# A hybrid RWKV-7 / sparse-attention / expert layer on one core: fewer gathered rows per v tile, more of them beside the weight matrix, eight low parts on GpSimd, four more unsplit v tiles

## The chip, the cores and the metric

The kernel runs on one core of one Trainium2 chip. The metric is device microseconds of one execution. Five engines run side by side, each through its own instruction stream in a fixed order: PE multiplies matrices, DVE, ACT and POOL (GpSimd) work on vectors, SP issues DMAs; POOL issues the gathering DMAs here as well. An instruction starts when those ahead of it in its stream have started and the semaphores that it waits for have come. A long wait at the head of a stream holds up everything behind it.

## The reference, cut to what matters

The layer has three parts: projections with RWKV-7 mixing and sparse attention, a gated output projection, and PEER, a layer of 16384 small experts. The change touches PEER alone:

```python
def block(hb):                       # 128 tokens
    q = (hb @ w_pq).reshape(PEER_BLOCK, PEER_HEADS, 2, PEER_DHALF)
    s = jnp.einsum('nhpd,hpkd->nhpk', q, peer_keys)
    ...                              # top 16 of 128 x 128 products of keys, by head
    e = jnp.take_along_axis(cidx, j, axis=-1)
    g = jax.nn.softmax(sc, axis=-1)
    act = jax.nn.gelu(jnp.einsum('nhkd,nd->nhk', peer_u[e], hb))
    return jnp.einsum('nhk,nhkd->nd', (g * act), peer_v[e])
```

There are 384 tokens of 1024 numbers. Each token has 8 heads of 16 chosen experts, 128 in all, and adds up 128 rows of `peer_v`, each weighted by a gate and by the gelu of a dot product with a row of `peer_u`.

## The kernel before

The 384 tokens are served in two ways at once.

**The sparse way** serves the 128 tokens of the sample group, one token a partition. In step q each token fetches its q-th expert: one indirect DMA, issued by POOL (L1603), brings 128 rows of 2048 numbers (u and v side by side, 1 MB). Here such a step is called a row. For each row DVE makes a dot product (L1610), ACT the gelu and the gate's factor (L1611, L1612), and DVE adds the scaled v half to an accumulator (L1616). There are 128 rows. They land in a ring of three buffers (`raw`), and late in the program also in parts of the large tile `G` that have become free.

**The dense way** serves the 256 prompt tokens with all experts, as if every token had chosen each of them with a weight that is mostly zero. The 16384 experts are 128 tiles of 128. For a u tile PE computes h2 times u (`dense_u`, L1501 on), ACT applies gelu. The weight matrix (`weights`, 64 groups of four tokens) is built from one-hot vectors by DVE and ACT and by small matmuls, and multiplied into the gelu values. For a v tile (`dense_v`) PE multiplies the weighted values with v and adds the result up in four banks `bx`, `cp`, `dx`, `dx` of PSUM over all 128 tiles.

A product in full precision goes to PE in one of two forms. Unsplit ("whole"), the operands are read as they are, and each matmul takes two passes. Split, ACT writes a rounded high part (`wh`, `Gh`; L238), another engine subtracts it for a low part (`wl`, `Gl`; L242), and PE makes three cheaper products, high x high, high x low and low x high. Of a v tile that is 12 matmuls of 512 columns, against 4 of two passes each.

The order around the change, in `run`:

- u tiles 0 to 41 unsplit, u tiles 42 to 75 split; from tile 30 on every tile pulls `SR[0]` = 0.5 rows.
- The weight matrix: 64 groups. After each group `ahead` (the step) makes half a u tile on average (`UR` = 0.5, tiles of the list `AHEAD`: 31 of the tiles from 76 on) and pulls `SR[1]` rows.
- 128 v tiles in an order that mixes early and late ones; their place is n. Before each, `SR[2]` rows are pulled; from n = 5 on a row may start only when the v tile five places ahead is done (`self.pace`, L1603's wait for PE). The 21 u tiles that are left go in between. A v tile is unsplit if n < 3, or if 8 < n < `EARLY` and n is divisible by 3.
- At n = 122 rows that are still left are pulled at once, and the sample tokens' result is written. The last two v tiles are finished bank by bank (`finish_v`), so that DVE can add the residual (L1586, L1587) of one bank while PE works on the next.

The order in which a program's instructions enter each engine's stream is set when the kernel is built, by a scheduler with a model of time of its own; so a change in one place moves instructions around it. The split's buffers are four for `wh`, three for `wl`, and three each for `Gh` and `Gl`.

Of the kernel before, what the change touches and what calls it, by code (L numbers as in the profile page):

```python
# [179 lines left out]

N1, NW, NA, NB = 42, 76, 8, 24
SCORES, TURNS = 18, (21, 39)
SR, UR = (0.5, 0.5, 0.62), 0.5
S0, PH = 30, 4
OFF = [j for j in range(NW, 128) if (j - NW + 1) * NB // (128 - NW) > (j - NW) * NB // (128 - NW)]
AHEAD = sorted(OFF + [j for j in range(NW, 128) if j not in OFF][:NA - 1])
LAST, EARLY = 126, 108
FREED = {}
for _k in "RWRWRWW":
    _a = max((j + 1 for j in FREED), default=0)  # L190
    FREED[_a + (7 if _k == "R" else 3)] = (_k, _a)
WB, EB = (4, 4, 3), 3
UENG, VENG, GENG, VN = 'v', 'v', 'g', 3
SENG = 'gv'
HENG, EENG, OB = 'va', 'vg', 3

# [5 lines left out]
class K:  # L202
# [1298 lines left out]
    def dense_u(self, j):  # L1501

        nc = self.nc
        u = self.expert(self.I["puT"][j].rearrange("p k e -> p (k e)"))
        p = self.ps([128, 256], tag="mm" if j < N1 and j % 2 else "u")
        if j < N1:
            u = u.rearrange("p (k e) -> p k e", k=8)
            for k in range(8):
                self.ulast = self.mm(p, u[:, k], self.h2f[:, k], start=(k == 0), stop=(k == 7))
        else:  # L1510
            uh, ul = (x.rearrange("p (k e) -> p k e", k=8) for x in self.split(u, UENG[j % len(UENG)]))
            hi, lo = self.h2p
            for k in range(8):
                self.mm(p, uh[:, k], hi[:, k], start=(k == 0), stop=False)
                self.mm(p, uh[:, k], lo[:, k], start=False, stop=False)
                self.mm(p, ul[:, k], hi[:, k], start=False, stop=(k == 7))
        off = j in OFF
        g = self.G[:, j] if j < NW else self.t([128, 256], tag="gO" if off else "gA", bufs=2 if off else NA, pool=self.late)
        nc.scalar.activation(g, p, AF.Gelu_apprx_tanh)
        if off:  # L1520
            nc.sync.dma_start(self.Ad[OFF.index(j)], g)
        return g
# [273 lines left out]
```

## Time and profile before

| | us |
|---|---|
| median of 3 runs | 1746.16 (1745.84 to 1750.6) |
| the profiled execution | 1751.29 |
| its span, first to last instruction | 1749.5 |
| one weight group's last instructions end, v tiles begin | about 1285 |
| last row is issued | 1693 |
| last matmul ends | 1744.7 |

The granted PE clock is 0.984 on average. Times below are microseconds from the start of the span. A line of groups reads: source line, engine, operation, what it writes and reads, shape, count, then busy time, mean nanoseconds of one, idle time of the engine just before them and what ended it. Most matmuls share L234, since one helper records them all; they are told apart by their tiles (`fx` of split u tiles, `bx`, `cp`, `dx` of v tiles).

### The profile page before, as it was taken

To read this page: it belongs to the slowest core of one execution; us is meant where nothing else is said; L and a number is where in the kernel's file an instruction comes from. 1 tells how busy PE (TensorE), PEld (TensorE's weight loads), DVE (VectorE), ACT (ScalarE), POOL (GpSimd) and SP (SyncE) were. 2 spreads that over 40 slices of the span, in tenths; PEclk is the share of its full clock that TensorE was granted. 3 is DMA by queue.
4 is the path that set the end of the run, shared out by engine and by line. 5 is a ranking of instruction groups with operands and counts; after the bars stand their busy time and mean duration, and the time that the engine had idled before them with its cause. 6 is when DMAs were issued, how large, how long until landed. Compare 5 with 4: busy or idle time off the path is not lost.

```text
span 1749.5 us, 33109 instructions
## 1 busy us (share of the span) xinstructions
PE 1671.5 (96%) x12376; PEld 1411.1 (81%) x12376; DVE 1358.9 (78%) x2905; ACT 744.2 (43%) x1666; POOL 550.2 (31%) x621
## 2 busy tenths in 40 slices
PE   6999899999999988999999989999999999999997
PEld 3998788878878877899887889999965776776675
DVE  3548888878858865566999998899957887777797
ACT  4443343333333333444323254577844433343343
POOL 2534243343323220035033223342233334332331
PEclk7999899999999999999999999999999999999999
DMA  8543653455365365755398989997579999999993
GB/s 294 171 133 104 195 177 89 146 173 158 103 202 157 98 210 178 261 184 195 126 358 320 366 322 372 390 330 242 175 257 357 380 385 370 392 394 375 351 396 111
DMA packets 173049, 437.23 MB, mean 250 GB/s; under 512 B 46036, under 2 KB 86612, under 8 KB 156504
## 3 DMA queue, kind: packets, MB, share of 16 engines
q1 hardware_dynamic: 154456, 300.89, 50.6%
q0 software_dynamic: 18432, 134.23, 19.8%
q8 instruction: 98, 1.61, 0.4%
q14 instruction: 63, 0.52, 0.1%
HBM read 403.75 MB, written 31.30 MB: 249 GB/s over the span
## 4 chain that ended last, share of the span: by engine, by line
PE 63%; DVE 17%; DMA 8%; issue 6%; ACT 3%; POOL 2%; SPq 0%; DVEq 0%; POOLq 0%; ACTq 0%
PE mm L234 23%; PE fx L234 12%; PE dx L234 11%; PE cp L234 7%; PE bx L234 7%; DVE acc L1616 2%; DVE wl L242 2%; DMA raw<-in_puv,pe 2%; DVE raw L1610 2%; DMA w<-in_w_in 1%; ACT wh L238 1%; DMA w<-in_puT 1%; POOL raw L1603 1%; DMA w<-in_pv 1%; DVE ps L1331 1%
## 5 line engine op out<-in xcount | busy, mean ns | idle before, releaser
L242 DVE TENSOR_TENSOR wl<-w,wh 128x1024 fp32r<-128x1024 f32 x231 | 291.5, 1266 | 94.3 <-ACT wh L238 55.3
L238 ACT ACTIVATE wh<-w 128x1024 fp32r<-128x1024 f32 x239 | 250.3, 1051 | 156.7 <-PE mm L234 70.9
L1603 POOL DMA_INDIRECT raw<-in_puv,pe x100 | 136.0, 1360 | 335.9 <-DVE acc L1616 118.0
L234 PE MATMUL fx<-h2h,wl 128*128 128x256 f32 x688 | 195.3, 285 | 3.9 <-DVE wl L242 3.8
L234 PE MATMUL fx<-h2h,wh 128*128 128x256 f32 x688 | 196.6, 286 | 0.9 <-ACT wh L238 0.7
L234 PE MATMUL fx<-h2l,wh 128*128 128x256 f32 x688 | 193.5, 281 | 0.0
L1616 DVE SCALAR_TENSOR_TENSOR acc<-raw,dots,acc 128x1024 f32<-128x1024 f32 x99 | 129.4, 1307 | 8.6 <-ACT dots L1612 8.5
L234 PEld LDWEIGHTS fx<-h2h,wl 128*128 128x128 f32 x688 | 130.3, 190 | 6.4 <-DVE wl L242 5.4
L234 PEld LDWEIGHTS fx<-h2h,wh 128*128 128x128 f32 x688 | 129.6, 188 | 5.6 <-ACT wh L238 2.7
L1610 DVE SCALAR_TENSOR_TENSOR raw<-raw,sh 128x1024 f32<-128x1024 f32 x100 | 125.4, 1254 | 7.4 <-DMA raw<-in_puv,pe 7.2
L234 PEld LDWEIGHTS fx<-h2l,wh 128*128 128x128 f32 x688 | 129.8, 189 | 1.6 <-issue 1.2
L234 PE MATMUL mm<-LTh,wh 128*128 128x384 f32 (+2 forms) x352 | 124.1, 353 | 2.1 <-ACT wh L238 1.5
L234 PE MATMUL mm<-LTh,wl 128*128 128x384 f32 (+2 forms) x352 | 123.2, 350 | 0.6 <-DVE wl L242 0.6
L234 PE MATMUL mm<-LTl,wh 128*128 128x384 f32 (+2 forms) x352 | 122.5, 348 | 0.0
L234 PE MATMUL mm<-h2f,w 128*128 128x256 f32 x464 | 105.4, 381 | 0.0
L1611 ACT ACTIVATE dots<-dots 128x1 f32<-128x1 f32 x128 | 25.4, 199 | 178.7 <-DVE raw L1610 149.5
L234 PE MATMUL mm<-wh,LTh 128*128 128x256 f32 x336 | 98.0, 292 | 1.7 <-ACT qx L898 1.7
L234 PE MATMUL mm<-wl,LTh 128*128 128x256 f32 x336 | 99.0, 295 | 0.0
L234 PE MATMUL mm<-wh,LTl 128*128 128x256 f32 x336 | 97.6, 290 | 0.0
L234 PEld LDWEIGHTS mm<-h2f,w 128*128 128x128 f32 x464 | 87.5, 190 | 12.4
L234 PE MATMUL fx<-h2f,w 128*128 128x256 f32 x336 | 78.3, 386 | 0.0
L234 PEld LDWEIGHTS mm<-LTh,wh 128*128 128x128 f32 (+2 forms) x352 | 66.7, 189 | 7.6 <-ACT wh L238 2.9
(609 smaller groups left out, 4475.8 us busy)
## 6 DMA issues: line engine op xcount, KB each, us to landing
w<-in_puT SPq DMA_DIRECT2D x119, 512.0 KB
w<-in_pv SPq DMA_DIRECT2D x85, 512.0 KB
w<-in_w_in SPq DMA_DIRECT2D x70, 512.0 KB
w<-in_w_ada SPq DMA_DIRECT2D x48, 512.0 KB
G<-in_pv SPq DMA_DIRECT2D x43, 512.0 KB
cKT<-in_cKT SPq DMA_DIRECT2D x32, 256.0 KB
cV<-in_cV SPq DMA_DIRECT2D x32, 256.0 KB
w<-in_w_pq SPq DMA_DIRECT2D x16, 512.0 KB
```

The source lines that it names most:

```text
L234: return self.nc.tensor.matmul(out, l, r, start=start, stop=stop, skip_group_check=True, **kw)
L238: self.nc.scalar.activation(hi, src, AF.Copy)
L242: (self.nc.vector if eng == "v" else self.nc.gpsimd).tensor_tensor(lo, src, hi, op=OP.subtract)
L1331: nc.vector.match_replace(out=s2, in_to_replace=sv[:, half, h, 0:8], in_values=s[:, c], imm_value=MARK)
L1603: d = nc.gpsimd.indirect_dma_start(out=bass.AP(tensor=u.tensor, offset=u.offset, ap=[u.ap[0], [1, 2048]]), out_offset=None, in_=self.I["puv"],
L1610: nc.vector.scalar_tensor_tensor(u, u, 1.0, h2, op0=OP.mult, op1=OP.mult, accum_out=dot)
L1611: nc.scalar.activation(dot, dot, AF.Gelu_apprx_tanh)
L1616: nc.vector.scalar_tensor_tensor(acc, v, dot, acc, op0=OP.mult, op1=OP.add)
```

## The change

Four numbers and one expression are changed. Rows beside the weight groups go from 0.5 to 0.57 a group, rows per v tile from 0.62 to 0.545. `EARLY` goes from 108 to 120, so the v tiles at n = 108, 111, 114 and 117 are no longer split. The low part of a split u tile is made by DVE before; now those at places 2, 6, 10 ... 30 of `AHEAD`, eight of 31, are made by POOL.

```diff
-SR, UR = (0.5, 0.5, 0.62), 0.5
+SR, UR = (0.5, 0.57, 0.545), 0.5
...
-LAST, EARLY = 126, 108
+LAST, EARLY = 126, 120
...
-UENG, VENG, GENG, VN = 'v', 'v', 'g', 3
+VENG, GENG, VN = 'v', 'g', 3
...
-            uh, ul = (x.rearrange("p (k e) -> p k e", k=8) for x in self.split(u, UENG[j % len(UENG)]))
+            uh, ul = (x.rearrange("p (k e) -> p k e", k=8) for x in self.split(u, "g" if j in AHEAD and AHEAD.index(j) % 4 == 2 else "v"))
```

The rows pulled in the program by the end of the weight groups are 55 before (6 with u tiles 30 to 41, 17 with tiles 42 to 75, 32 with the groups) and 59.48 now. The first five v tiles pull without a wait for PE: 58.1 before, 62.2 now.

On POOL's stream beside the weight groups, `G<-G,wg` (L1433) multiplies a group's weights into the gelu values, `raw<-in_puv,pe` (L1603) issues a row, `wl` (L242) is a low part. Before:

```order
L1603 DMA raw_15224<-in_puv,pe_2057_10521 128x2048
L1433 TENSOR_TENSOR G_11076<-G_11076,wg_13467 128x76x4
L1603 DMA raw_15258<-in_puv,pe_2057_10521 128x2048
L1433 TENSOR_TENSOR G_11076<-G_11076,wg_13533 128x76x4
L1603 DMA raw_15284<-in_puv,pe_2057_10521 128x2048
L1433 TENSOR_TENSOR G_11076<-G_11076,wg_13600 128x76x4
L1603 DMA raw_15303<-in_puv,pe_2057_10521 128x2048
L1433 TENSOR_TENSOR G_11076<-G_11076,wg_13673 128x76x4
L1603 DMA raw_15332<-in_puv,pe_2057_10521 128x2048
L1433 TENSOR_TENSOR G_11076<-G_11076,wg_13740 128x76x4
```

The same place of POOL's stream now:

```order
L1603 DMA raw_14920<-in_puv,pe_2057_10521 128x2048
L242 TENSOR_TENSOR wl_13268<-w_13264,wh_13267 128x1024
L1433 TENSOR_TENSOR G_11076<-G_11076,wg_13407 128x76x4
L1603 DMA raw_14987<-in_puv,pe_2057_10521 128x2048
L1433 TENSOR_TENSOR G_11076<-G_11076,wg_13474 128x76x4
L1603 DMA raw_15061<-in_puv,pe_2057_10521 128x2048
L242 TENSOR_TENSOR wl_13548<-w_13544,wh_13547 128x1024
L1603 DMA raw_15118<-in_puv,pe_2057_10521 128x2048
L1433 TENSOR_TENSOR G_11076<-G_11076,wg_13540 128x76x4
L1433 TENSOR_TENSOR G_11076<-G_11076,wg_13607 128x76x4
L1603 DMA raw_15185<-in_puv,pe_2057_10521 128x2048
```

The low parts stand right behind row issues, so they start after whatever those wait for.

On DVE's stream at the end of the program, L1610 and L1616 are the two halves of a row, L242 the low parts of v tiles (`wl`) and of their weighted values (`Gl`), L1586 the residual. Before, the last row is followed by five v tiles' low parts:

```order
L1616 SCALAR_TENSOR_TENSOR acc_11701<-G_11076,dots_18511,acc_11701 128x1024
L1586 TENSOR_TENSOR G_11076<-acc_11701,G_11076 128x512 x2
L242 TENSOR_TENSOR wl_18631<-w_18628,wh_18630 128x1024
L242 TENSOR_TENSOR Gl_18704<-G_11076,Gh_18703 128x256
L242 TENSOR_TENSOR wl_18676<-G_11076,wh_18675 128x1024
L242 TENSOR_TENSOR wl_18700<-G_11076,wh_18699 128x1024
L242 TENSOR_TENSOR wl_18721<-G_11076,wh_18720 128x1024
L242 TENSOR_TENSOR Gl_18728<-gB_18724,Gh_18727 128x256
L242 TENSOR_TENSOR Gl_18751<-gA_18028,Gh_18750 128x256
L242 TENSOR_TENSOR wl_18746<-w_18743,wh_18745 128x1024
L242 TENSOR_TENSOR wl_18756<-G_11076,wh_18755 128x1024
L242 TENSOR_TENSOR Gl_18763<-gB_18759,Gh_18762 128x256
```

Now the last three rows stand among the low parts of the last two v tiles:

```order
L242 TENSOR_TENSOR wl_18682<-w_18679,wh_18681 128x1024
L242 TENSOR_TENSOR Gl_18687<-gA_18009,Gh_18686 128x256
L1610 SCALAR_TENSOR_TENSOR G_11076,dots_18547<-G_11076,sh_2289_11699 128x1024
L242 TENSOR_TENSOR wl_18692<-G_11076,wh_18691 128x1024
L1616 SCALAR_TENSOR_TENSOR acc_11701<-G_11076,dots_18547,acc_11701 128x1024
L1610 SCALAR_TENSOR_TENSOR G_11076,dots_18575<-G_11076,sh_2289_11699 128x1024
L1610 SCALAR_TENSOR_TENSOR G_11076,dots_18581<-G_11076,sh_2289_11699 128x1024
L1616 SCALAR_TENSOR_TENSOR acc_11701<-G_11076,dots_18575,acc_11701 128x1024
L1616 SCALAR_TENSOR_TENSOR acc_11701<-G_11076,dots_18581,acc_11701 128x1024
L242 TENSOR_TENSOR Gl_18699<-gB_18695,Gh_18698 128x256
L1586 TENSOR_TENSOR raw_18587<-acc_11701,raw_18586 128x512 x2
```

The last v tile's `wl` and `Gl` were next to each other; five instructions of three rows stand between them now, and the sample group's residual comes behind both.

## The prediction

> **What bounds the kernel now.** The page comes first: PE is busy for nearly the whole span, so an edit gains only where PE waits, and costs wherever it gives PE work.
>
> ```profile
> span 1749.5 us, 33109 instructions
> PE 1671.5 (96%) x12376; PEld 1411.1 (81%) x12376; DVE 1358.9 (78%) x2905; ACT 744.2 (43%) x1666; POOL 550.2 (31%) x621
> ```
>
> Then the table by stage, for the stretch that the change touches: the weight groups in two halves, the start of the v tiles, their body, and the last 20 v tiles. Columns: start and end, length, busy time of PE, PEld, DVE, ACT and POOL with counts, granted clock, DMA share, GB/s.
>
> ```profile
> 1137.00:1210.00 73.00, 71.26 (x612) 70.42 (x611) 72.90 (x94) 54.81 (x140) 26.30 (x18) 1.00 0.84 299
> 1210.00:1285.00 75.00, 72.38 (x602) 69.54 (x600) 65.96 (x101) 63.86 (x176) 18.21 (x19) 1.00 0.51 173
> 1285.00:1360.00 75.00, 69.25 (x294) 48.00 (x295) 48.91 (x59) 26.76 (x55) 30.52 (x26) 1.00 0.93 351
> 1360.00:1677.00 317.00, 314.16 (x1359) 225.99 (x1358) 249.22 (x292) 123.71 (x253) 107.33 (x87) 1.00 0.99 379
> 1677.00:1750.00 73.00, 60.95 (x247) 46.38 (x245) 61.14 (x72) 30.84 (x59) 17.16 (x12) 0.97 0.59 223
> ```
>
> Three different limits show. Beside the weight groups PE and DVE are both full; DVE has 0.1 us idle in the first half and 9.0 in the second. In the v tiles' body PE is full and the DMA engines are full as well, at 379 GB/s. In the last stretch neither PE nor DMA is full, and DVE is the busiest.
>
> Third, PE's waits, by groups. In the v tiles from 1292.6 to 1677.2 those groups before which PE stood still are:
>
> ```profile
> L234 PE MATMUL fx<-h2h,wh 128*128 128x256 f32 x167 | 49.1, 294 | 0.7 <-ACT wh L238 0.7
> L234 PE MATMUL fx<-h2h,wl 128*128 128x256 f32 x168 | 48.1, 286 | 0.8 <-DVE wl L242 0.8
> ...
> L234 PE MATMUL bx<-wh,Gh 128*128 128x512 f32 x72 | 37.4, 520 | 3.1 <-ACT wh L238 3.1
> L234 PE MATMUL bx<-wl,Gh 128*128 128x512 f32 x72 | 29.4, 408 | 2.1 <-DVE wl L242 1.9
> ...
> L234 PE MATMUL bx<-w,gB 128*128 128x512 f32 x10 | 5.2, 598 | 1.7 <-DMA w<-in_pv 1.7
> ```
>
> Together 8.4 us in 385 (0.7 + 0.8 + 3.1 + 2.1 + 1.7). So DMA, though full, hardly delays PE. From 1677.3 on, where 20 v tiles are left, all split:
>
> ```profile
> L234 PE MATMUL bx<-wl,Gh 128*128 128x512 f32 x20 | 9.0, 449 | 1.9 <-DVE wl L242 1.7
> L234 PE MATMUL bx<-wh,Gh 128*128 128x512 f32 x20 | 8.4, 420 | 4.8 <-ACT wh L238 4.8
> ```
>
> That is 6.7 us of waits, and one of them has a tail:
>
> ```profile
> 1711.51 0.66 PE L234 MATMUL bx<-wh,Gh 128*128 128x512 f32 x1 [1.78 <-ACT wh L238]
> ...
> 1713.25 0.63 PE L234 MATMUL bx<-wl,Gh 128*128 128x512 f32 x1
> 1713.67 0.63 PE L234 MATMUL cp<-wl,Gh 128*128 128x512 f32 x1
> ...
> 1715.95 0.39 PE L234 MATMUL bx<-wh,Gh 128*128 128x512 f32 x1
> ...
> 1718.67 0.39 PE L234 MATMUL bx<-wh,Gh 128*128 128x512 f32 x1
> ```
>
> A full split tile takes 1718.67 - 1715.95 = 2.72 us, 0.227 a matmul. After the wait of 1.78 us matmuls start 0.42 apart, and the tile that began at 1711.51 takes 4.44: 1.7 more. Waits and slow tile make 8.4 us of the last stretch.
>
> **The change part by part**, against the profiled execution's 1751.29 us; the median of the runs is 5.1 lower, and I take that off at the end.
>
> *Four unsplit v tiles.* An unsplit tile has four matmuls of two passes, one for each bank:
>
> ```profile
> 1636.63 1.02 PE L234 MATMUL bx<-G,gA 128*128 128x512 f32 x2
> 1637.48 1.02 PE L234 MATMUL cp<-G,gA 128*128 128x512 f32 x2
> ```
>
> One bank takes 0.85, a tile 3.42, which is 0.70 more than a split one: **+2.8** for PE over the four. Nothing hides this, since PE is the bound on both sides of it. What it takes from DVE is the low parts, of a whole tile and of its values:
>
> ```profile
> L242 DVE TENSOR_TENSOR Gl<-G,Gh 128x256 fp32r<-128x256 f32 x53 | 24.9, 472 | 29.7 <-ACT dots L1611 12.0 <-PE dx L234 9.8 <-ACT Gh L238 7.9
> ...
> L242 DVE TENSOR_TENSOR wl<-w,wh 128x1024 fp32r<-128x1024 f32 x231 | 291.5, 1266 | 94.3 <-ACT wh L238 55.3
> L1616 DVE SCALAR_TENSOR_TENSOR acc<-raw,dots,acc 128x1024 f32<-128x1024 f32 x99 | 129.4, 1307 | 8.6 <-ACT dots L1612 8.5
> L1610 DVE SCALAR_TENSOR_TENSOR raw<-raw,sh 128x1024 f32<-128x1024 f32 x100 | 125.4, 1254 | 7.4 <-DMA raw<-in_puv,pe 7.2
> ```
>
> That is 4 x (1.27 + 0.47) = 7.0 us of DVE.
>
> *Rows moved.* Of the 128 rows 58 are pulled before the pace begins, 62 now: four rows leave the v tiles. On DVE a row costs 1.25 + 1.31 = 2.56, so 10.2 us go from the v tiles to the weight groups; with them go four L1603 on POOL, and 4.2 MB, 11 us of DMA at 379 GB/s. PE waits for only 8.4 us there, 1.7 of it for a DMA by name, so the 11 us cannot come back whole. Bounds: 0 and -8.4. I take **-3**, near the 1.7 and part of the 3.1 behind `wh`, which itself waits for tiles to land.
>
> *Low parts on GpSimd.* The trace has eight of them, early in the program, and shows what one does to DVE (minimum, median, maximum in ns; then three pieces of the timeline):
>
> ```profile
> L242 POOL TENSOR_TENSOR wl<-w,wh x8: 2353/2406/3383, 79.7 to 824.6; 128x1024 fp32r<-128x1024 f32 x8
> ...
> 807.89 0.42 DVE L1250 TENSOR_TENSOR modr<-ga,pah 128x256 f32<-128x256 f32 x1
> ...
> 813.73 2.60 DVE L1250 TENSOR_TENSOR h<-ga,pah 128x256 f32<-128x256 f32 x1
> ...
> 813.69 2.35 POOL L242 TENSOR_TENSOR wl<-w,wh 128x1024 fp32r<-128x1024 f32 x1 [1.57 <-ACT wh L238]
> ```
>
> An instruction that takes 0.42 alone took 2.60 when GpSimd's 2.35 had begun 0.04 before it: DVE stood still for its whole length. So eight low parts take 8 x 1.27 = 10.1 us off DVE and can put up to 8 x 2.35 = 18.8 back. Some will fall beside instructions that are not held up, or GpSimd will be the one that waits; I take half, 9.4. DVE then gains 0.7 and pays 10.2 for the rows: +9.5 against 9.1 idle in the two halves. A low part also stands behind row issues, which wait for a ring buffer:
>
> ```profile
> POOL raw L1603 <- DVE acc L1616: 15.1, 5, 4.9
> ...
> L234 PE MATMUL fx<-h2h,wl 128*128 128x256 f32 x247 | 70.4, 286 | 1.4 <-DVE wl L242 1.4
> ```
>
> Five waits of 3.0 on average; behind them PE's `fx<-h2h,wl`, which waits for 1.4 us in these stretches now, would wait longer, with three `wl` buffers as its cushion. Bounds: with no hold-up and a full cushion the stage gains that 1.4; with every low part held up in full, DVE has 18.9 to fit into 9.1 and the stage grows by 10. I take **+3**, nearer to the former since the rows spread into the half with room.
>
> The Trainium skill, "SBUF — State Buffer", section "Who interferes with whom", says that a VectorE instruction with two SBUF inputs and a GpSimd instruction that reads SBUF exclude each other, and that the second one blocks fully. The row at 813.73 agrees. By that rule alone moving work to GpSimd would bring DVE no time at all: the sum would have 18.8 in place of 9.4, the second rival's.
>
> *The end.* From the start of the last 20 tiles (n = 108) DVE adds nine more rows before:
>
> ```profile
> L1616 DVE SCALAR_TENSOR_TENSOR acc<-raw,dots,acc 128x1024 f32<-128x1024 f32 x5 | 6.9, 1375 | 0.0
> L1616 DVE SCALAR_TENSOR_TENSOR acc<-G,dots,acc 128x1024 f32<-128x1024 f32 x4 | 5.6, 1396 | 0.1
> ```
>
> So 119 are done there before; now, by 118.3 pulled through n = 107 and a lag of two to three, about 116. Three more rows, 7.7 us, balance the 7.0 saved, so DVE stays the busiest there, but the load shifts back: ten tiles with less, ten with more. Of the 8.4 us I let **-6** go. At the very end the order now has five row instructions between the last tile's `wl` and `Gl`. Before:
>
> ```profile
> 1724.99 1.29 DVE L1586 TENSOR_TENSOR G<-acc,G 128x512 f32<-128x512 f32 x2
> ...
> 1736.15 1.23 DVE L242 TENSOR_TENSOR wl<-G,wh 128x1024 fp32r<-128x1024 f32 x1 [0.17 <-PE dx L234]
> 1737.30 0.42 DVE L242 TENSOR_TENSOR Gl<-gB,Gh 128x256 fp32r<-128x256 f32 x1
> ...
> 1740.21 0.39 PE L234 MATMUL bx<-wh,Gl 128*128 128x512 f32 x1
> ...
> 1740.63 0.69 DVE L1586 TENSOR_TENSOR raw<-bx,raw 128x512 f32<-128x512 f32 x1 [2.92 <-PE bx L234]
> ...
> 1745.44 0.69 DVE L1587 TENSOR_TENSOR raw<-raw,raw 128x512 f32<-128x512 f32 x1
> ```
>
> That `wl` starts when PE lets its buffer go, three split tiles before, so it cannot come sooner. Five instructions of about 1.2 push `Gl` from 1737.30 to 1743.4, its end to 1743.8. PE uses it at 1740.21: a wait of 3.6. DVE then has the sample group's residual (1.3) before 5.5 us of the last residuals (1740.63 to 1746.1), ending at 1750.6: +4.5. A wait of that length may halve the clock as at 1711.51; 18 matmuls follow, up to 3.5, partly behind DVE's queue. I take **+5** (bounds +2, if PE is late by itself, and +11).
>
> The sum: 2.8 - 3 + 3 - 6 + 5 = +1.8, 1753.1 in this execution's terms, **1748.0** in the median's.
>
> **The rivals.** *Faster: the waits go.* If what PE waits for in the v tiles is DMA at bottom, 11 us less of it takes 7 of the 8.4; if the relieved DVE frees all 8.4 of the last stretch and the end costs only 2, and the groups nothing: 2.8 - 7 - 8.4 + 2 = -10.6, 1735.6. For it: DMA at 0.99. Against it: PE is busy 314 of 317 there.
>
> *Slower: GpSimd holds DVE.* In the weight groups every low part stops DVE for its length, DVE becomes the bound and PE waits for `wl`. The stage grows by 10, not 3: 1755. It decides once a low part holds DVE for more than 1.2 us on average, since then the idle 9.1 are used up. For it: 813.73 and DVE's 72.90 of 73. Against: the second half has 9.0 free.
>
> *Slower: the last rows land late.* The last three rows wait for the v tile at n = 117, where the last one waited for n = 112. Three rows are 3.1 MB, 8.3 us at 379 GB/s, behind what is under way (up to six ring buffers and eight v tiles, some 20 us). They have about seven tiles, 19 us. Landing 6 us late makes it 1754. For it: rows now run to the end of the stretch. Against: the DMA share of 0.59 there.
>
> **How the numbers follow.** The forecast, within 0.3% (5.2 us, about what a measurement here can tell from no change): 0.42. Faster: 0.26. GpSimd: 0.18. Late rows: 0.14. Both slower cases end 6 to 9 above the median, so slower has 0.32. The range reaches from 1737, which leaves out about half of the faster case, to 1759, which takes in each slower case alone and leaves out a sum of the two.
>
> **What would show it.** In the new profile: about 62 L1603 before the v tiles; PE's waits of 1292 to 1677 at 5 rather than 8.4; DVE instructions of over 2 us beside POOL's eight `wl`; PE's last wait, for `Gl` or `Gh` behind the rows' L1610, near 3.6. The forecast is wrong if the v tiles' body shortens by more than 5, or the weight groups lengthen by more than 6.

## The result and the profile after

The changed kernel takes 1760.99 us (median of six runs, 1757.27 to 1766.18) against 1746.27 (six runs, 1744.72 to 1750.6): a ratio of 1.0084, interval 1.0064 to 1.0105. It is slower, and 13 us above the forecast of 1748. The profiled execution took 1766.18, the slowest of the six, and 14.9 us more than that of before; the traces below are compared with this in mind.

The page of the changed kernel, the same two lines as before (span; busy time, share and instructions of each engine):

```profile
span 1764.4 us, 33043 instructions
PE 1682.1 (95%) x12360; PEld 1417.2 (80%) x12360; DVE 1351.9 (77%) x2889; ACT 737.4 (42%) x1658; POOL 559.8 (32%) x629
```

DVE has 7.0 us less to do in all, and PE 10.6 more. The table by stage says where (columns as before: PE, PEld, DVE, ACT, POOL, granted clock, DMA share, GB/s); the four rows are the weight groups in two parts, the v tiles' body and the last stretch:

```profile
1140.00:1213.00 73.00, 65.97 (x546) 64.20 (x545) 72.73 (x84) 50.91 (x137) 35.25 (x25) 0.98 0.83 296
1213.00:1307.00 94.00, 82.83 (x670) 79.48 (x668) 81.39 (x117) 69.34 (x189) 33.81 (x25) 0.96 0.54 189
1312.80:1687.60 374.80, 374.20 (x1641) 272.40 (x1640) 275.67 (x325) 145.15 (x292) 123.17 (x104) 1.00 0.98 366
1687.60:1764.40 76.80, 65.85 (x229) 46.44 (x227) 60.20 (x75) 26.71 (x57) 19.94 (x17) 0.89 0.70 262
```

Two stages moved in opposite directions. In the weight groups PE now stands still (65.97 of 73 and 82.83 of 94), with the granted clock below 1.00. In the body PE no longer does: 374.20 of 374.80 (this window begins 1.9 us ahead of the body as it is measured below).

To compare kernels whose stages begin at different times, each stage is measured between events: the weight groups from the third `wst` (L1434) to the first matmul of the v tile n = 3 (so with the first three v tiles), the body from there to the first matmul of n = 108, then to that of n = 126, then to PE's end.

| us | start of groups | groups | body | n = 108 to 126 | 126 to PE's end | to the end of the span | span |
|---|---|---|---|---|---|---|---|
| before | 1137.7 | 155.0 | 384.7 | 61.7 | 5.6 | 4.8 | 1749.5 |
| after | 1141.0 | 173.6 | 372.9 | 59.8 | 12.3 | 4.8 | 1764.4 |
| difference | +3.3 | **+18.6** | **-11.8** | -1.9 | **+6.7** | 0 | +14.9 |

The start of the groups lies ahead of all that the change touches; in the kernels below it falls anywhere from 1133 to 1145, whatever their edits, so the +3.3 is scatter.

What PE waited for in the weight groups after (for whom, total, times, longest):

```profile
PE mm L234 <- DVE oh L1421: 4.3, 1, 4.3
PE cp L234 <- DVE oh L1421: 3.7, 3, 2.0
PE fx L234 <- DVE wl L242: 3.2, 5, 1.7
PE bx L234 <- DVE oh L1421: 2.5, 2, 1.5
```

and the two largest before:

```profile
PE fx L234 <- DVE wl L242: 1.4, 1, 1.4
PE cp L234 <- ACT oh L1473: 1.4, 1, 1.4
```

All four are waits for DVE, and three of the four are for one-hot vectors, which are no part of the change. They come late because DVE does. Its groups of instructions there, after:

```profile
L1421 DVE TENSOR_TENSOR oh<-wA,wB 128x512 f32<-128x512 f32 x55 | 47.1, 878 | 2.9 <-issue 2.7 <-ACT gO L1519 0.2
L242 DVE TENSOR_TENSOR wl<-w,wh 128x1024 fp32r<-128x1024 f32 x26 | 34.5, 1333 | 2.8 <-ACT wh L238 0.9 <-issue 0.9 <-PE fx L234 0.8
L1616 DVE SCALAR_TENSOR_TENSOR acc<-raw,dots,acc 128x1024 f32<-128x1024 f32 x14 | 21.2, 1512 | 0.0
L1468 DVE TENSOR_TENSOR oh<-pT,dx 128x512 f32<-128x512 f32 x27 | 18.3, 676 | 0.0
...
L1433 DVE TENSOR_TENSOR G<-G,mm 128x304 f32<-128x304 f32 x32 | 14.7, 461 | 2.4 <-PE mm L234 2.4
```

and before:

```profile
L242 DVE TENSOR_TENSOR wl<-w,wh 128x1024 fp32r<-128x1024 f32 x34 | 42.9, 1273 | 2.4 <-ACT wh L238 2.1 <-issue 0.2
L1421 DVE TENSOR_TENSOR oh<-wA,wB 128x512 f32<-128x512 f32 x55 | 42.1, 783 | 1.9 <-ACT wst L1434 1.3 <-issue 0.2 <-ACT oh L1473 0.2
L1468 DVE TENSOR_TENSOR oh<-pT,dx 128x512 f32<-128x512 f32 x27 | 18.3, 677 | 0.2 <-PE bx L234 0.2
L1433 DVE TENSOR_TENSOR G<-G,mm 128x304 f32<-128x304 f32 x32 | 14.7, 462 | 0.8 <-PE mm L234 0.8
L1616 DVE SCALAR_TENSOR_TENSOR acc<-raw,dots,acc 128x1024 f32<-128x1024 f32 x10 | 13.3, 1334 | 0.0
```

The eight low parts did leave (34 to 26), but the same 55 one-hot instructions take 95 ns more each, and the rows' additions 178. L1468 and L1433 stay as they were. They read one operand from PSUM, the memory for matmul results (`dx`, `mm`), and that they were not held up is no accident of place: four L1433 (457 to 470 ns) and one L1468 (675 ns) ran wholly beside a low part of GpSimd. The instructions that grew read both operands from SBUF, the on-chip memory that GpSimd reads as well. One place in the timeline where the two engines held each other up (start, length, what it waited for), on GpSimd and on DVE:

```profile
1234.59 3.51 POOL L242 TENSOR_TENSOR wl<-w,wh 128x1024 fp32r<-128x1024 f32 x1 [3.61 <-ACT gO L1519]
...
1234.54 1.28 DVE L1616 SCALAR_TENSOR_TENSOR acc<-raw,dots,acc 128x1024 f32<-128x1024 f32 x1
1235.74 2.51 DVE L1447 SCALAR_TENSOR_TENSOR wab<-wab,pT 128x128 bf16<-128x128 bf16 x1
```

The instruction at 1235.74 has 128 columns and ends at 1238.25, after GpSimd's low part has ended at 1238.10. Each of the two is longer than it would be alone: the low part's shortest in this trace is 2.36 us, and L1447 takes 0.29 in the kernel with GpSimd alone (e2, below), where no low part stands beside it. The low part had begun 0.05 behind an L1616 of DVE, which ended at 1235.82 at its usual length. So the low part lost that time first, and the next DVE instruction then waited for the low part.

In the body all that is left of PE's waits is one line, where there were five with 8.4 us:

```profile
PE bx L234 <- ACT wh L238: 0.4, 1, 0.4
```

At the end, PE and then DVE:

```profile
1747.77 0.39 PE L234 MATMUL bx<-wh,Gl 128*128 128x512 f32 x1
1750.03 0.50 PE L234 MATMUL bx<-wh,Gh 128*128 128x512 f32 x1 [1.88 <-ACT Gh L238]
1750.37 0.40 PE L234 MATMUL bx<-wl,Gh 128*128 128x512 f32 x1
1752.10 0.80 PE L234 MATMUL bx<-wh,Gl 128*128 128x512 f32 x1 [1.33 <-DVE Gl L242]
1752.69 0.63 PE L234 MATMUL cp<-wh,Gh 128*128 128x512 f32 x1
1753.12 0.63 PE L234 MATMUL cp<-wl,Gh 128*128 128x512 f32 x1
```

```profile
1744.40 1.23 DVE L242 TENSOR_TENSOR wl<-G,wh 128x1024 fp32r<-128x1024 f32 x1
...
1749.03 2.68 DVE L1616 SCALAR_TENSOR_TENSOR acc<-G,dots,acc 128x1024 f32<-128x1024 f32 x2
1751.63 0.42 DVE L242 TENSOR_TENSOR Gl<-gB,Gh 128x256 fp32r<-128x256 f32 x1
```

`Gl` stands behind the rows, as its place in the order says. PE waits 1.88 + 1.33 = 3.2 us, and from 1752.10 on its matmuls start 0.43 apart, where 0.23 is the full rate.

### The profile page after: what moved, and what is told of

It is laid out like the page before. It is cut to its first block, busy times and chain, and to the rows that moved or that the text cites. A ratio compares the mean times of both kernels' runs of the same rounds, so it can differ in the third digit from the quotient of the medians.

```text
span 1764.4 us, 33043 instructions
## 1 busy us (share of the span) xinstructions
PE 1682.1 (95%) x12360; PEld 1417.2 (80%) x12360; DVE 1351.9 (77%) x2889; ACT 737.4 (42%) x1658; POOL 559.8 (32%) x629
## 4 chain that ended last, share of the span: by engine, by line
PE 65%; DVE 18%; DMA 8%; issue 5%; ACT 3%; POOL 2%; SPq 0%; DVEq 0%; POOLq 0%; ACTq 0%
PE mm L234 23%; PE dx L234 13%; PE fx L234 10%; PE cp L234 8%; PE bx L234 7%; DVE acc L1616 3%; DVE raw L1610 2%; DVE wl L242 2%; DMA raw<-in_puv,pe 2%; DMA w<-in_puT 2%; DMA w<-in_pv 1%; ACT wh L238 1%; DMA w<-in_w_ada 1%; DVE oh L1421 1%; DMA w<-in_w_in 1%
## 5 line engine op out<-in xcount | busy, mean ns | idle before, releaser
L242 DVE TENSOR_TENSOR wl<-w,wh 128x1024 fp32r<-128x1024 f32 x222 | 277.9, 1256 | 93.4 <-ACT wh L238 53.7
L1603 POOL DMA_INDIRECT raw<-in_puv,pe x100 | 134.5, 1345 | 371.4 <-DVE acc L1616 139.8
L1616 DVE SCALAR_TENSOR_TENSOR acc<-raw,dots,acc 128x1024 f32<-128x1024 f32 x99 | 130.4, 1318 | 8.1 <-ACT dots L1612 8.0
L1610 DVE SCALAR_TENSOR_TENSOR raw<-raw,sh 128x1024 f32<-128x1024 f32 x100 | 126.2, 1262 | 9.5 <-DMA raw<-in_puv,pe 9.5
```

The costliest lines, as they stand in the source:

```text
L242: (self.nc.vector if eng == "v" else self.nc.gpsimd).tensor_tensor(lo, src, hi, op=OP.subtract)
L1603: d = nc.gpsimd.indirect_dma_start(out=bass.AP(tensor=u.tensor, offset=u.offset, ap=[u.ap[0], [1, 2048]]), out_offset=None, in_=self.I["puv"],
L1610: nc.vector.scalar_tensor_tensor(u, u, 1.0, h2, op0=OP.mult, op1=OP.mult, accum_out=dot)
L1616: nc.vector.scalar_tensor_tensor(acc, v, dot, acc, op0=OP.mult, op1=OP.add)
```

## The experiments

Stage lengths come from one profiled execution of each kernel. Where an edit touches nothing of a stage, the groups repeat within 154.2 to 155.3, but for 157.9 in e10, and the body within 382.4 to 386.1, but for 390.8 in e7. Times and ratios are against runs of the kernel before on the same chip.

### The change in its parts

`e1` is the changed kernel without GpSimd's low parts, the other three are the kernel before with one part each:

```diff
e1: after, with   self.split(u, "v")
e2: before, with  self.split(u, "g" if j in AHEAD and AHEAD.index(j) % 4 == 2 else "v")
e3: before, with  SR, UR = (0.5, 0.57, 0.545), 0.5
e4: before, with  LAST, EARLY = 126, 120
```

> The changed kernel with all low parts on DVE again: rows and the four unsplit tiles stay. Theory A (eight GpSimd low parts hold DVE up beside the weight groups, 1.8 us each, and PE then waits for one-hot vectors): that stage falls from 166 us to 152 or less, the v tiles keep their 373 us and the tail its 72; about 1745, that is 0.998 to 1.001 of the kernel before. Theory B (the four rows, which DVE does ahead of one-hot vectors, fill the stage): it stays above 160 us and the time at 1755 or more.

> The kernel before with only the eight low parts on GpSimd. Theory A: DVE loses 15 us and is spared 10 in a stage where it has 9 idle; PE waits some 5 to 9 us more: 1751 to 1756. Theory B: DVE is relieved or even, 1744 to 1748.

> The kernel before with only the rows moved. Theory A: the weight groups take 2 to 5 us more, the v tiles to n = 107 10 less, the tail 4 to 6 more since the last rows stand ahead of the last low part: 1742 to 1747. Theory B: the groups take 12 or more, 1752 or more.

> The kernel before with only the four further unsplit v tiles. PE gains 2.8 us of work, DVE is spared 7.0 and ACT about 6 in the tail, where PE waits for them 8.4 us: 1742 to 1747. If the tail's waits come from the order alone, +3 and 1749.

| | time, us | ratio to before | groups | body | 108 to 126 | 126 to PE's end |
|---|---|---|---|---|---|---|
| before | 1749.21 | | 155.0 | 384.7 | 61.7 | 5.6 |
| e1, rows and unsplit tiles | 1752.72 | 1.0037 (1.0018 to 1.0056) | 164.2 | 373.3 | 59.8 | 12.9 |
| e2, GpSimd alone | 1759.70 | 1.0070 (1.0048 to 1.0092) | 162.8 | 386.1 | 60.5 | 5.6 |
| e3, rows alone | 1749.29 | 1.0001 (0.9987 to 1.0014) | 163.9 | 373.3 | 54.8 | 10.7 |
| e4, unsplit tiles alone | 1749.45 | 1.0003 (0.9987 to 1.0018) | 154.7 | 383.8 | 59.7 | 5.6 |

GpSimd's low parts cost 10.5 us alone (1759.70 - 1749.21), most of the change's 14.7. Its profiled execution was the fastest of its six, and shows 7.8 of them in the groups. The rows alone cost nothing in sum: they lengthen the groups by 8.9, shorten the body by 11.4, the last two stretches go from 67.3 to 65.5, and what comes behind PE's end from 4.8 to 7.7 (that profiled execution, 1757.66, was the slowest of twelve). So neither theory of e1 and e3 holds: theory A took the rows in the groups for nearly free, theory B for nearly all of it, and rows and low parts lengthen the groups about equally. The two causes in the groups nearly add up: 7.8 + 8.9 = 16.7 of 18.6. The unsplit tiles are free alone; beside the moved rows the last two stretches take 72.7 instead of 65.5 (78.1 instead of 73.2 to the end of the span).

### What in GpSimd's work holds DVE up

Two kernels leave all low parts on DVE and give GpSimd other work at the same eight places, whose result is overwritten later: `e7` three subtractions of 128x256, `e8` nine fills with a constant, which read nothing.

```diff
+            if probe:
+                for c in range(3):
+                    nc.gpsimd.tensor_tensor(g, u[:, c * 256:c * 256 + 256], u[:, 768:], op=OP.subtract)
e8 instead:
+                for c in range(9):
+                    nc.gpsimd.memset(g, float(c))
```

> The kernel before, in which GpSimd makes three more subtractions of 128x256 beside the weight groups at eight places, the same tiles of which the change takes the low part; DVE still makes all low parts, and what GpSimd writes is overwritten later. Theory L (GpSimd instructions that read the on-chip memory stop DVE for their length): 24 subtractions of about 0.6 us put 10 to 15 us on DVE's instructions there, and the groups grow from 155.0 to 162 or more. Theory Q (what held PE up is that a low part waits in GpSimd's stream behind row issues): the groups stay within 155 to 157, since no one waits for these instructions.

> As the run with GpSimd's subtractions, at the same eight places, but with nine fills of 128x256 with a constant each, which read nothing from the on-chip memory. Theory L with two kinds (only instructions that read stop DVE): the groups stay at 155 to 157, however long the fills last. Theory L without kinds (any GpSimd instruction stops DVE): 72 fills of at least 0.2 us lengthen the groups by 6 or more. Theory Q: they stay at 155 to 157, or grow where the rows' issues behind the fills come late, which the idle time before DVE's dot products would show.

Times 1760.93 (ratio 1.0081, 1.0052 to 1.0110) and 1747.56 (0.9997, 0.9978 to 1.0015). The stage of the groups by windows, before, with the subtractions, with the fills (columns as in the table by stage):

```profile
1137.70:1292.70 155.00, 150.38 (x1224) 142.65 (x1222) 138.97 (x194) 118.90 (x317) 44.63 (x38) 1.00 0.67 234
```

```profile
1133.70:1297.80 164.10, 153.14 (x1220) 145.20 (x1219) 146.40 (x195) 118.52 (x316) 73.44 (x62) 0.98 0.62 217
```

```profile
1137.20:1293.00 155.80, 150.28 (x1223) 142.65 (x1222) 138.36 (x194) 119.68 (x316) 62.94 (x100) 1.00 0.67 232
```

With the subtractions the groups take 9.1 us more, and DVE is busy 7.4 us longer with the same instructions, less than the 10 to 15 expected. The run's time grew by more, 14.0; in its profile the body is 6.1 us longer as well (see the last section). GpSimd's 24 subtractions took this much:

```profile
L1516 POOL TENSOR_TENSOR gO<-w 128x256 f32<-128x256 f32 x24 | 27.2, 1133 | 8.9 <-DMA d<-gO 7.8
```

The fills, some 20 us of GpSimd as well, leave DVE and the stage as they were. Seven of their eight places lie beside the groups, as all eight of the subtractions do (the scheduler moved the first nine fills to 1023). What waits for either is the gelu that overwrites their tile, 4.4 us for the subtractions and 0.6 for the fills, so a part of the stage's 9.1 may come through ACT; DVE's 7.4, put on its own instructions, does not. So it is not the place in the stream: reading is what holds DVE up. The Trainium skill, "SBUF — State Buffer", section "Who interferes with whom", says just this of a VectorE instruction with two SBUF inputs: it contends with a GpSimd instruction that reads SBUF, not with one that only writes it. The two runs agree, 7.4 against -0.6 us of DVE.

The length of one hold-up follows from the same view of the kernel with GpSimd alone:

```profile
1133.50:1296.20 162.70, 150.47 (x1221) 142.24 (x1221) 146.34 (x187) 118.15 (x315) 63.11 (x47) 1.00 0.66 223
```

DVE gives up eight low parts, 10.1 us, and is still busy 7.4 longer: 17.5 us put on the rest, 2.2 a low part.

### Why the body became shorter

The body issues fewer rows than the prediction counted. The issues (L1603, on POOL) in it, before and after, with POOL's busy time and their count:

```profile
1292.60:1677.20 384.60, 83.88 (x66) 1.00 0.99 377
```

```profile
1312.80:1687.60 374.80, 75.61 (x58) 1.00 0.98 366
```

Eight left, not four: four go ahead of it, four behind it. Four experiments on the kernel before take parts of rows out of the body; a row that is not fetched also saves its issue on POOL and its ring buffer:

```diff
e5:  no fetch (no buffer, no indirect DMA) for the rows 68, 80, 92, 104
e6:  the same rows are fetched, then
+                if q * PH * 16 + j in (68, 80, 92, 104):
+                    yield
+                    continue
e12: as e5, for range(64, 112, 6), eight rows
e15: neither fetched nor added, for range(64, 112, 6)
```

> The kernel before, in which the rows 68, 80, 92 and 104 of the gathered rows, all pulled in the v tiles' body, fetch nothing: their DVE and ACT instructions work on the rows fetched ahead of them, so the sums of the sample tokens are not the reference's. The transfers of four rows (4.2 MB, 11 us at 379 GB/s) are taken away, DVE's work stays. Theory D (the body's 11.8 us came from the DMA engines, whose transfers set when the tiles land): the body from v tile n = 3 to n = 108 shortens from 384.7 to 375 or less. Theory V (they came from DVE, which makes the low parts sooner with four rows less): it stays at 383 to 386. Outside the body nothing changes by either.

> The kernel before, in which the same four rows 68, 80, 92 and 104 are fetched, but the dot product, the gelu and the adding of them are left out, so the sums of the sample tokens are not the reference's. DVE's work of four rows (4 x 2.56 = 10.2 us) is taken away, the transfers stay. Theory V: the body from n = 3 to n = 108 shortens from 384.7 to 375 or less. Theory D: it stays at 382 to 386. If both this run and the one without the transfers shorten it by half, neither alone is the limit.

> The kernel before, in which eight rows of the body (64, 70, 76 ... 106) fetch nothing, and DVE and ACT work on the rows fetched ahead of them, so the sums of the sample tokens are not the reference's. Four rows so treated shortened the body by 4.6 us. Theory D, that the changed kernel's body is 11.8 us shorter because it has eight rows fewer issued in it (58 against 66), expects 372 to 377. Theory S (the effect saturates: only part of the slack is the transfers'): 379 to 381, as with four.

> The kernel before, in which the eight rows 64, 70, 76 ... 106 are left out altogether, neither fetched nor added, so the sums of the sample tokens are not the reference's. Without their transfers alone the body was 8.4 us shorter. If the other 3.4 of the changed kernel's 11.8 are DVE's work of those rows, the body is now 371.5 to 374; if DVE's work counts for nothing there, 375 to 378, and the other 3.4 come from where the rows that are left stand.

| | time, us | ratio to before | body, us | against before |
|---|---|---|---|---|
| e5, four not fetched | 1743.31 | 0.9972 (0.9955 to 0.9990) | 380.1 | -4.6 |
| e6, four not added | 1750.13 | 1.0011 (0.9988 to 1.0033) | 384.8 | +0.1 |
| e12, eight not fetched | 1736.58 | 0.9934 (0.9912 to 0.9956) | 376.3 | -8.4 |
| e15, eight left out | 1734.56 | 0.9924 (0.9902 to 0.9946) | 374.5 | -10.2 |

The expectation for e5, 375 or less, was too much, since it too took four rows for the whole effect. Four transfers give 4.6, eight give 8.4, and DVE's work of four rows nothing. Eight rows' work beside the transfers may give another 1.8, which is within the body's own scatter; the last 1.6 of the 11.8 is not accounted for. The body before, with eight rows not fetched, and with eight left out:

```profile
1292.70:1677.40 384.70, 376.37 (x1637) 270.93 (x1636) 297.36 (x348) 149.80 (x306) 137.03 (x112) 1.00 0.99 377
```

```profile
1289.50:1665.80 376.30, 373.95 (x1637) 271.53 (x1636) 295.46 (x349) 150.22 (x308) 122.81 (x105) 1.00 0.96 361
```

```profile
1289.10:1663.60 374.50, 373.79 (x1636) 271.48 (x1635) 275.74 (x325) 147.24 (x292) 125.20 (x105) 1.00 0.97 364
```

With eight rows not fetched PE is idle for 2.4 us instead of 8.3, and busy for 374.0 instead of 376.4 with the same matmuls. The shortest body of all runs, 371.7 in e11, has PE busy throughout and is about its floor. Most of what stood above that in the kernel before was there because of transfers, though PE's waits named mostly ACT and DVE. How a transfer gets to delay PE is not shown: ACT's own idle time for tiles to land is 17.2 us in the body before, and 20.7 in e12.

### The rows elsewhere

```diff
e9:  after,  pull(SR[2] if n < 108 else 1.0)
e10: before, SR, UR = (0.5, 0.5, 0.58), 0.5    and   pull(SR[2] if n < 108 else 1.0)
e11: before, SR, UR = (0.6, 0.5, 0.545), 0.5   and   pull(SR[2] if n < 108 else 1.0)
e13: before, SR, UR = (0.5, 0.5, 0.65), 0.5
e14: before, SR, UR = (0.5, 0.44, 0.68), 0.5
```

> The changed kernel with one number more: from v tile n = 108 on 1.0 row is pulled per v tile instead of 0.545, so that the last rows are added before the low parts of the last two v tiles. Theory E (the end is late because the last values' low part stands behind five row instructions on DVE): the stretch from n = 126 to PE's end returns from 12.3 us to 5.6, no matmul of it runs at half rate, and the run is 5 to 8 us faster than the changed kernel unless the stretch from 108 to 126 takes it back (59.8 in the changed kernel; 60 to 62 expected). Theory T (DVE has more to do than it can in the last 20 tiles, wherever the rows stand): the end gets shorter, but 108 to 126 longer by as much.

> The kernel before, in which only the v tiles' rows are moved: 0.58 per v tile instead of 0.62 up to n = 107 and 1.0 from there on; the weight groups keep their 0.5, no other part of the change is in it. Four rows leave the body for the last 20 v tiles. Theory D (a row's transfer costs the body 1.1 to 1.4 us): the body shortens from 384.7 to 379 to 381, the groups stay at 155, and if DVE in the last 20 tiles has room for 10 us more the run is 3 to 6 us faster than before. Theory T (it has not): the stretch from 108 to the end grows by 4 or more and the run is the same as before.

> As the run with the rows moved to the end, but four rows more leave the body, for the dense u tiles ahead of the weight groups: 0.6 a u tile instead of 0.5, 0.545 per v tile, the groups keep 0.5. The body then has eight rows less, as in the changed kernel: 372 to 375 by theory D. Four rows beside u tiles, where PE hardly waits, cost nothing if DVE and the transfers have room there (start of the groups at 1134 to 1140 as before), and the run is 8 to 14 us faster than before; if DVE or the transfers, at 0.91 to 1.00 of their engines, hold PE up there, the groups start 5 to 9 us later and the gain is 0 to 6.

> The kernel before with 0.65 rows per v tile instead of 0.62, nothing else: the opposite direction. The body gets three rows more, the last 20 v tiles three fewer, the weight groups stay. Theory P (a row has a price by stage: 1.1 us in the body, where its transfer counts, 2.2 beside the groups and about 2.5 in the last 20 tiles, where DVE counts): the body grows to 387 to 389, the last stretch (n = 108 to PE's end, 67.3 before) falls to 60 to 63, and the run is 1 to 5 us faster than before. If DVE does not set the last stretch, it stays at 66 to 68 and the run is 3 us slower.

> The kernel before with 0.44 rows a weight group instead of 0.5 and 0.68 per v tile instead of 0.62, so that about four rows leave the groups and the body gets seven more; the last 20 tiles are as in the run with 0.65. Theory P with PE as the groups' floor (PE is busy for all but 5 us of them): the groups shorten from 155.0 to 150 to 153, not by 4 times 2.2; the body grows to 391 to 394; the run is as long as before or up to 4 us longer. Without that floor the groups shorten to 146 and the run is 3 to 5 us faster than before.

Rows are counted by their issues ahead of, in and behind the body; 58, 66 and 4 in the kernel before, 62, 58 and 8 in the changed one.

| | ratio to before | rows | groups | body | 108 to PE's end |
|---|---|---|---|---|---|
| e9 | 1.0065 (1.0045 to 1.0086) | 62, 60, 6 | 173.1 | 373.2 | 65.0 + 6.9 |
| e10 | 1.0071 (1.0046 to 1.0096) | 58, 63, 7 | 157.9 | 382.7 | 65.3 + 12.9 |
| e11 | 1.0033 (1.0016 to 1.0051) | 62, 60, 6 | 164.4 | 371.7 | 62.0 + 11.2 |
| e13 | 1.0068 (1.0051 to 1.0086) | 58, 70, 0 | 154.2 | 393.8 | 60.0 + 5.6 |
| e14 | 1.0052 (1.0034 to 1.0071) | 55, 72, 1 | 148.9 | 397.7 | 58.3 + 5.6 |

Each direction costs. *Into the body*: four rows more make it 9.1 us longer, six more 13.0, 2.2 to 2.3 a row (with eight fewer it was 1.1 to 1.4). The body with four more:

```profile
1290.50:1684.30 393.80, 379.62 (x1637) 271.97 (x1635) 305.94 (x358) 151.45 (x314) 142.72 (x116) 1.00 0.98 376
```

PE stands still for 14.2 us there. *Out of the groups*: e14 gains 6.1 of the stage, and PE is busy 147.6 of its 148.9 us, so the floor lies somewhat lower than the 150 to 153 expected; but the body takes 13 for it. *Ahead of the groups*: pulling four rows more beside the u tiles moved none there. In e11, as in before, 49 rows have been added by the start of the groups, and 13 are added beside them, as in the changed kernel; the groups grow by 9.4 though their own rate is that of before.

*To the end*: e10 was expected to gain 3 to 6 us, or by its second theory nothing; it lost 12 (0.0071 of 1748.44; 13.3 by the medians). In e9 the last two tiles' stretch shrinks from 12.3 to 6.9, and the one ahead of it grows from 59.8 to 65.0: the sum is 71.9 instead of 72.1. PE's waits there, for whom, total, times, longest:

```profile
PE bx L234 <- ACT wh L238: 4.1, 4, 1.1
PE bx L234 <- DVE wl L242: 3.7, 4, 1.7
```

By ratio e9 can't be told from the changed kernel, and no version here is clear of noise faster than the kernel before, except those that leave rows out.

### What sets the last 20 tiles

DVE's load was the first theory for this (T); e13, with three rows fewer there, should by it have come down to 60 to 63 and came to 65.6, from 67.3. The second was ACT's order. In e9, all engines, at a tile's end:

```profile
1726.37 0.61 PE L234 MATMUL dx<-wh,Gl 128*128 128x512 f32 x2
1726.57 0.42 ACT L238 ACTIVATE Gh<-G 128x256 fp32r<-128x256 f32 x1 [2.32 <-PE dx L234]
1726.90 1.04 ACT L238 ACTIVATE wh<-w 128x1024 fp32r<-128x1024 f32 x1
...
1727.99 0.50 PE L234 MATMUL bx<-wh,Gh 128*128 128x512 f32 x1 [1.00 <-ACT wh L238]
```

ACT's `Gh` waits for PE to finish the tile whose buffer it takes, the `wh` that PE needs next stands behind it in ACT's stream, and PE runs dry. With another number of buffers that wait should go:

```diff
-        gh, gl = (self.t([128, 256], F32R, tag=tag, bufs=3) for tag in ("Gh", "Gl"))
+        gh, gl = (self.t([128, 256], F32R, tag=tag, bufs=4) for tag in ("Gh", "Gl"))
e16: before with 4;   e21: e9 with 4;   e20: e9 with 2
```

> The kernel before with four buffers each for Gh and Gl instead of three, nothing else. Theory O (the last 20 tiles are set by the order on ACT: a tile's high part wh stands in ACT's stream behind a Gh of a later tile, and that Gh waits until PE has finished the tile three places before it, so PE gets wh only after it has run dry): a Gh waits for one tile less, PE's waits for wh from n = 108 on fall from 4.8 us to 2 or less, the stretch from n = 108 to PE's end falls from 67.3 to 62 to 65, and the run is 0 to 4 us faster than before. Theory T (DVE's load sets it): it stays at 66 to 68.

> The changed kernel with the last rows pulled at 1.0 per v tile, and with four buffers each for Gh and Gl. With three, PE waited 4.1 us for wh in the last 20 tiles, 1.0 to 1.1 before each of four tiles, and these tiles took 4.4 us instead of 2.72. Theory O: those waits go, and the stretch from n = 108 to PE's end falls from 71.9 to 62 to 67. Theory T: it stays at 70 or more, with PE waiting for wl on DVE instead.

> The same with two buffers each for Gh and Gl: in ACT's order a tile's wh now stands ahead of the Gh of the next but one, and a Gh waits for the tile two places before it. Theory O: PE's waits for wh in the last 20 tiles fall as well, since what counts is what wh stands behind, not how many buffers there are: 62 to 68 from n = 108 to PE's end. If the number of buffers counts, the waits grow and the stretch is longer than 72.

| | ratio to before | n = 108 to PE's end | body |
|---|---|---|---|
| e16 | 1.0029 (1.0018 to 1.0040) | 67.6 (before 67.3) | 391.5 |
| e21 | 1.0118 (1.0094 to 1.0142) | 75.2 (e9 71.9) | 376.8 |
| e20 | 1.0091 (1.0073 to 1.0109) | 69.6 (e9 71.9) | 374.7 |

Neither theory stands. With four buffers the kernel before has the same waits for `wh` as with three, 4.7 us:

```profile
PE bx L234 <- ACT wh L238: 4.7, 4, 1.7
PE bx L234 <- DVE wl L242: 1.7, 1, 1.7
```

ACT's `Gh` still waits there for PE, once for 3.0 us, probably because the scheduler moves `Gh` forward along with the buffer; so in this pair the edit did not take away what it was meant to. With two buffers (e20) the stretch came out between what the theories allowed. What sets this stretch stays open; shown is only that neither three rows of DVE, nor the place of the last rows, nor the buffers of `Gh` bring it near the 2.72 us a tile.

## Why the prediction was wrong

The result lies above the range, on the side of the rival "GpSimd holds DVE". That rival had the mechanism right. Its price was too low: the groups were to grow by 10, rows included, and grew by 18.6. That its time, 1755, is off by no more than 6 is luck, since the body shrank by 11.8 as well, and so is the nearness of its 10 to the 10.5 that the low parts cost without the rows. The forecast's sum failed in three of its terms, against +15.6, -8.8 and +3.0 us; the second hides a part of the first.

**Low parts on GpSimd, +3: the step that failed.** The hold-up was taken at half of the low part's length, "since some will fall beside instructions that are not held up": 9.4 us, 1.2 each. Measured, it is 17.5 alone (2.2 each), and so DVE gained nothing by giving the work away and lost 7.4. The row quoted in the prediction (0.42 us become 2.60) had shown the full length already, and the threshold given for the rival, 1.2 us a low part, was passed. The other half of this term was the room in the groups: the 9.1 us of DVE's idle time in two windows of 148 were counted as usable. Rows alone show that they are not: DVE was busy 9.0 longer (148.02 in the row below, 138.97 before), and the stage grew by 8.9.

```profile
1144.80:1308.70 163.90, 151.94 (x1209) 142.64 (x1208) 148.02 (x207) 120.33 (x323) 55.55 (x41) 0.99 0.68 242
```

DVE's idle time (16.0 of 155 before, 15.9 here) stayed what it was. So the stage paid for both parts in full, +18.6 where its upper bound stood at +10. The cushion of `wl` buffers, on which the lower bound rested, mattered little: of PE's waits listed above 10.5 us are for one-hot vectors in DVE's own stream and 3.2 for `wl`.

**Rows moved, -3: a term mis-sized.** Measured -11.8, below its bound of -8.4. Three readings failed. The rows that leave the body were counted as the four that go to the groups; four more go behind n = 108, which the prediction saw in its term for the end ("three more rows") but did not take off here. Of the idle time that PE's waits name, 8.4 us, only 3 were given to the transfers, the 1.7 put down to a DMA and a part of the 3.1 behind `wh`; e12, by transfers alone, takes 6.0 of PE's 8.3 us of idle time. And the bound was that idle time alone, as if PE's busy time were fixed: in the changed kernel's body PE is idle for 0.6 us, and busy for 372.3 where the same matmuls took 376.4 before. That a late tile delays `wh` on ACT, and that `wl` on DVE, is the likely way from a transfer to these waits, but it is argued and not shown. With e12 the first rival's reason was right ("if what PE waits for in the v tiles is DMA at bottom"), while the argument held against it, PE busy 314 of 317, was the share of time and no floor.

**Unsplit tiles, waits of the tail, the end: 2.8 - 6 + 5 = +1.8, measured +4.8** (72.1 against 67.3). These were right in kind. From n = 108 to 126 the forecast is 2.8 - 6 = -3.2, and -1.9 was measured, with a wait of 2.9 us for `wh` left, behind which matmuls start 0.43 apart. The end, +5, took 6.7, within its bounds of 2 and 11: PE waited 3.2 us where 3.6 were forecast, for `Gh` and `Gl`, and more of it than assumed ran at half rate. What sets the tail's waits is open, as the last experiments show. That the +2.8 are paid for by waits that go agrees with e4, where four unsplit tiles change the time by nothing that can be measured. Beside the moved rows they are not free: from n = 108 to the end of the span e1 takes 4.9 us more than e3.

**The rival of late last rows** is not what happened: what PE waits for last is `Gl` behind rows whose DVE instructions follow each other without a gap from 1744.40 to 1751.63, so their data was there.

**What would show it.** The prediction's two conditions for being wrong both came true: the body shortened by more than 5, the groups lengthened by more than 6. Of its other signs, the 62 rows ahead of the body, the DVE instructions of over 2 us and a last wait near 3.6 (3.2) came; PE's waits in the body fell to 0.4 and not to 5. The GpSimd term makes most of the miss: without it, e1 is 0.37% slower (0.18 to 0.56), at the edge of what the forecast called no change.

## What to carry to other kernels

Work moved off a full DVE to GpSimd gained nothing here, since GpSimd's instructions read the on-chip memory beside DVE instructions with both inputs there; look first at what both read. A single row in the trace that shows an instruction stretched to GpSimd's length is to be taken at its full price. Where the DMA engines are full, test the stage by leaving out transfers before trusting the engine that PE's waits name, and count what a rate moves at both ends of the stage. When work is shifted between stages that are each full in another resource, price a unit of it in every stage: here a row costs 1.5 to 2.2 us beside the groups and 1.1 to 2.3 in the body, so moving rows had nothing to give.

## What the runs showed of the hardware that was not expected

- PE's clock halved after some waits and not after others of nearly the same length. The granted clock was 0.62 behind a wait of 1.78 us (before, 1711.5 to 1716) and 0.50 behind waits of 1.88 and 1.33 with two matmuls between (after, 1752.1 to 1758); there matmuls ran 0.42 to 0.43 us apart. It stayed at 1.00 behind waits of 1.73 (e9, from 1742.8) and 1.75 (e13, from 1720.1), and in e9 after a wait of 1.00 us only two single matmuls of the tile were slower, at 0.33 and 0.34.
- When a GpSimd and a DVE instruction held each other up, both records grew: the low part's from 2.36 to 3.51 us, the 128-column DVE instruction's to 2.51. DVE instructions with one operand in PSUM were not held up.
- Two kernels whose edits add no row and no transfer to the body, e7 and e16, had it at 390.8 and 391.5 us, where before, e4, e6 and e8 have 382.4 to 384.8. In both PE has longer single waits there (2.8 and 3.2 us for `wh`, 1.7 at most before), and the granted clock is 0.98 and 0.99 where it is 1.00 before. What makes these waits is open.
